# Attention stage of a two-layer trunk: value differences from PSUM, keys of two heads split at once, residual sums issued a unit later, low output parts ahead of a blanking

## Chip, cores, metric

The kernel runs on one core of a Trainium2 chip. The metric is the device time of one execution in microseconds, lower is better. Engines are named as in the profile: PE (matrix multiply), PEld (its weight load), DVE (vector), ACT (scalar), POOL (GpSimd), SP (the engine that here only issues DMAs).

## The reference

Two layers, float32, one batch of 1024 tokens, width 1024. Layer 0 mixes tokens with a short gated convolution, layer 1 with sliding-window attention; a SwiGLU block of 2816 hidden units follows each. The change lies in layer 1's attention:

```
q, k, v = split(rmsnorm(x) @ w_qkv)                  # 16 query heads, 4 key/value heads, 64 wide
q, k = rmsnorm(q), rmsnorm(k)                        # per head
for each block of 128 queries, against its own and the previous block of keys:
    s = q @ k.T / 8 - slope[head] * distance         # only 0 <= distance < 128
    p = softmax([s, sink[head]])[:-1]
    o = p @ v
x = x + o @ w_o
```

## The kernel before

All products are float32 in three passes: an operand is split into a high part (rounded to the matmul format) and a low part (what is left), and high*high, high*low and low*high are added in PSUM. PE has nearly no pause from end to end; everything else is arranged around it. The order of the instructions on each engine is written by hand: `line.work(n, f)` appends PE work and advances a planned clock `line.end`; `line.at(t, f)` puts an action of another engine (or a DMA) at planned time t. When the program is recorded, actions come out in the order of t, and each engine runs its own in that order; a planned time is never waited for.

The attention runs in 32 units, `unit(u)`: block of queries b = u // 4, half of the heads c = u // 2 % 2, key head g = u % 2 within it. A unit holds the stages of three units at once, so that PE always has something to do:

- `scores(u)` on PE into the PSUM bank `twin`; `merge`, `bias`, `least` on DVE; `exponents` on ACT; `inverse` (reciprocal of the sum) on DVE; `normal` (the product with the reciprocal) on POOL.
- `turn(u-1)`: PE transposes the probabilities, so it needs `normal(u-1)`. Then `turn_hi` (ACT), `turn_lo` (DVE), and `select` (POOL, the "blanking": four `affine_select`, two on the high part, two on the low part).
- `values(u-2)` and `other_values(u-2)` on PE: the probabilities times v of one block, and the blanked ones times the difference of v between this block and the one before. Then `o_copy` (ACT) and `o_add` (DVE).
- `o_hi` (ACT) and `o_lo` (POOL): the split of finished outputs, needed only in the output product after the units.

Between these, PE works on pieces of three matmuls: the query and key/value projections of later blocks, and from unit 24 on the output product (`tail_piece`). Eight pieces make an output tile m; it ends in `tail_item`, which adds the tile to X (loaded again by `load_again` from unit 27 on), squares it (ACT), stores it (a DMA issued by POOL) and sums the squares (DVE).

For a block b, `dv_sum` made the difference v(b) - v(b-1) in `scratch()` from the split parts, in three POOL instructions spread over units 4b-3 to 4b-1; `dv_hi`, `dv_lo` and `dv_twice` split it in unit 4b and copied it to the other 64 partitions. For the keys of two heads, `key_turn` (PE) transposes them to 128 partitions, 64 for each head; `key_hi` and `key_lo` split each head by itself, and `key_twice` copies each to the other 64 partitions.

Of the kernel before, what the change touches and what calls it, by code (L numbers as in the profile page):

```python
# [12 lines left out]
AF = mybir.ActivationFunctionType  # L13
ALU = mybir.AluOpType
# [56 lines left out]
def trunk_kernel(ctx: ExitStack, tc: tile.TileContext, xT, small, table, w_in, w_out, w_kv, w_q, w_o, w_gu, w_dn, out):  # L71
# [38 lines left out]
    def plain(ap):  # L110
        return ap.bitcast(F32)
# [676 lines left out]
    class Line:  # L788
# [216 lines left out]
    def channel_mixer(layer, next_stage, src_of, operands, raw_tags, extra_tags, slots, line, lead_in):  # L1005
# [61 lines left out]
        def tail_item(h, m, k0=0):  # L1067
            c = slice(h * HALF, h * HALF + HALF)
            tail_part(h, m, range(k0, n_op))
            get = tails[h, m][1]  # L1070
            t = line.end

            def square():
                if layer and h == 0 and m == 0:
                    units["sq"] = slot("A2", (P, 3, HALF))
                if m == 0:
                    state["ss", h] = units["sq"][:, 2] if layer and h == 0 else slot(f"s{h}", (P, HALF))
                    act.activation(state["ss", h], X[m][:, c], AF.Square)
                else:
                    if layer and h == 0:  # L1080
                        units["sq", h, m] = units["sq"][:, m % 2]
                    else:
                        units["sq", h, m] = slot(f"G{10 + m % 2}", (P, HALF))
                    act.activation(units["sq", h, m], X[m][:, c], AF.Square)

            at(t + 0.05, lambda: dve.tensor_tensor(X[m][:, c], get(), X[m][:, c], ALU.add))
            at(t + 0.8, square)
            at(t + 0.9, lambda: nc.gpsimd.dma_start(xres[m][:, c], X[m][:, c]))
            if m:
                at(t + 1.6, lambda: dve.tensor_tensor(state["ss", h], state["ss", h], units["sq", h, m], ALU.add))  # L1090


        B, put = operands_of(line, slots)
# [460 lines left out]
    def attention_layer(line, mixer):  # L1554
# [150 lines left out]
        def scratch():  # L1705
            return side_room(0)[:, NKV * HD :].rearrange("p (g d) -> p g d", d=HD)
# [56 lines left out]
        def key_hi(b, c, g):  # L1763
            rows = slice(g * HD, (g + 1) * HD)
            act.activation(key_rooms(c)[rows, g, 0, b % 2, :], KT[b, c][rows, 0:P], AF.Copy, scale=state["qkg"][rows])

        def key_lo(b, c, g):
            rows = slice(g * HD, (g + 1) * HD)
            kz = key_rooms(c)
            dve.scalar_tensor_tensor(  # L1770
                kz[rows, g, 1, b % 2, :],
                KT[b, c][rows, 0:P],
                state["qkg"][rows],
                plain(kz)[rows, g, 0, b % 2, :],
                ALU.mult,
                ALU.subtract,
            )

        def key_twice(b, c, g):
            rows, rest = slice(g * HD, (g + 1) * HD), slice((1 - g) * HD, (2 - g) * HD)  # L1780
            kz = key_rooms(c)
            nc.sync.dma_start(plain(kz)[rest, g, :, b % 2, :], plain(kz)[rows, g, :, b % 2, :])


        def dv_sum(b, i):
            d, v, w = scratch(), plain(v_room(b + 1)), plain(v_room(b))
            if i == 0:
                pool.tensor_tensor(d, v[:, :, 0, :], w[:, :, 0, :], ALU.subtract)
            elif i == 1:
                pool.tensor_tensor(d, d, v[:, :, 1, :], ALU.add)  # L1790
            else:
                pool.tensor_tensor(d, d, w[:, :, 1, :], ALU.subtract)

        def v_down(b, n=HD):
            nc.sync.dma_start(plain(v_room(b))[0:n], plain(v_room(b + 1))[0:n])
# [218 lines left out]
        def lead_in(tail_part, tail_item):  # L2014
# [4 lines left out]
            for b in (0, 1):  # L2019
                d = t + (-0.6, 0.1)[b]  # L2020
                at(d, kv_v_hi, b)
                at(d + 0.5, kv_v_lo, b)
                if b == 0:
                    at(d + 1.5, v_down, 0, P)
                at(d + 1.0, kv_square, b)
# [21 lines left out]
            def turn_keys(b, c, t_hi, t_lo):  # L2047
                line.work(small_turn, key_turn, b, c)
                t_hi = line.end + 0.05 if t_hi is None else t_hi
                t_lo = line.end + 0.5 if t_lo is None else t_lo  # L2050
                for g in (0, 1):
                    at(t_hi, key_hi, b, c, g)
                    at(t_lo, key_lo, b, c, g)
                    at(t_lo + 0.6, key_twice, b, c, g)

            def turn_query(m, t_hi, t_lo):
                line.work(4 * small_turn, q_turn, m)
# [42 lines left out]
            def unit(u, last):  # L2100

                s = line.end
                n, g = u // 2, u % 2
                b, c = n // 2, n % 2
                todo = deque(fill[u] if u < NU else [])
# [38 lines left out]
                if 0 <= u - 2 < NU:  # L2144
                    if u - 2 >= 4:
                        line.work(4 * 0.27, other_values, u - 2)
                    at(line.end + 0.05, o_copy, u - 2)
                    at(max(line.end + 0.7, s + 4.0), o_add, u - 2)
                    if g == 1:
                        at(s + 6.7, o_hi, n - 1)  # L2150
                        if n - 1 < 14:
                            at(s + 6.5 + 5.0, o_lo, n - 1, (0, 1))
                            at(s + 13.0 + 5.0, o_lo, n - 1, (2, 3))
                        else:
                            at(s + 7.6, o_lo, n - 1)
                if 4 <= u - 1 < NU:
# [20 lines left out]
                if g == 1 and n < 12 and n % 2:  # L2177
                    kb = n // 2 + 2
                    for d, f in (
                        (3.55, kv_v_hi),  # L2180
                        (4.9, kv_v_lo),
                        (6.0, kv_square),
                        (6.4, kv_sum),
                        (7.0, kv_mean),
                        (7.1, kv_guess),
                        (7.6, kv_newton),
                        (6.5 + 5.2, kv_scale),
                    ):
                        at(s + d, f, kb)
                if b + 1 < NB and u % 4:  # L2190
                    at(s + 4.9, dv_sum, b + 1, u % 4 - 1)
                if b and u % 4 == 0:
                    at(s + 0.2, v_down, b)
                    at(s + 0.3, dv_hi, b)
                    at(s + 4.6, dv_lo, b)
                    at(s + 6.4, dv_twice, b)


            def load_again(m):
# [127 lines left out]
```

## Time and profile before

| | us |
|---|---|
| median of 3 runs | 1902.4 (1902.19 to 1902.78) |
| the profiled execution, its own time | 1902.64 |
| its span, first to last instruction | 1900.9 |
| attention units, start of unit 0's scores to start of unit 31's | 988.8 to 1194.6 |

In the rows of the profile, L1937 is `turn`, L1977 `other_values`, L1968 `values`, L1888 `scores`, L1845 the transposes of the queries that stand ahead of `turn` in even units, L1653 to L1655 a projection piece, L1061 to L1063 an output piece; on POOL L1931 is `normal`, L1959 `select`, L2011 `o_lo`, L1788 to L1792 `dv_sum`, L1807 its half of `dv_lo`; on DVE L1927 is `inverse`, L1731 `kv_v_lo`, L1086 the addition to X, L1090 the sum of squares, L1856 `q_lo`, L1998 `o_add`. A time row has start, duration, engine, line, operation, tiles, shape and count; the bracket is idle time before it and what ended it. A matmul of 512 columns is shown 0.39 us long, but the next one starts some 0.23 us after it: PE is read by starts.

### The profile page before, as it was taken

What the parts mean: (1) busy time and instruction counts of PE and PEld (TensorE: products, weight loads), DVE (VectorE), ACT (ScalarE), POOL (GpSimd) and SP (SyncE); (2) the same over time, 40 slices, a digit from 0 to 9 for tenths busy, and PEclk for the clock granted to TensorE, in tenths of its full rate; (3) what the DMA queues carried; (4) which work ended last, traced back from release to release, by engine and by line L of the source; (5) the groups of instructions that cost most, each with busy time, mean ns of one, the idle gap of its engine ahead of it and who ended that gap; (6) DMA issues with size and microseconds to landing.
All of it is one profiled execution on the core that took longest, in us unless ns stands there. A gap on an engine that the chain in (4) does not pass through costs nothing.

```text
span 1900.9 us, 24865 instructions
## 1 busy us (share of the span) xinstructions
PE 1891.5 (100%) x8603; PEld 1567.9 (82%) x8603; DVE 1372.0 (72%) x2233; ACT 852.2 (45%) x1710; POOL 330.4 (17%) x634
## 2 busy tenths in 40 slices
PE   9999999999999999999999999999999999999999
PEld 7888888888888888888888887888888888888887
DVE  8997878868777777766678888468767676765543
ACT  5543444523333344444557777335333333344441
POOL 0000011012222221000016777300111111100000
PEclk9999999999999999999999999999999999999999
DMA  8522176146666667987730115744454654477563
GB/s 312 174 95 78 67 293 216 60 168 225 218 229 214 224 208 244 359 292 235 239 115 22 25 38 171 280 168 138 150 188 150 215 188 162 165 282 263 196 228 101
DMA packets 160254, 351.38 MB, mean 185 GB/s; under 512 B 15936, under 2 KB 60352, under 8 KB 160000
## 3 DMA queue, kind: packets, MB, share of 16 engines
q1 hardware_dynamic: 133632, 256.83, 40.4%
q0 software_dynamic: 26208, 92.81, 13.4%
q8 instruction: 67, 1.10, 0.2%
q14 instruction: 59, 0.48, 0.1%
q10 hardware_dynamic: 288, 0.16, 0.0%
HBM read 241.34 MB, written 103.28 MB: 181 GB/s over the span
## 4 chain that ended last, share of the span: by engine, by line
PE 90%; POOL 3%; DVE 3%; ACT 2%; issue 1%; DMA 1%; SPq 0%; DVEq 0%; POOLq 0%; ACTq 0%
PE acc L946 16%; PE acc L947 16%; PE acc L948 16%; PE P L946 9%; PE P L947 9%; PE P L948 9%; PE acc L1061 2%; PE acc L1062 2%; PE acc L1063 2%; PE acc L175 1%; PE P L1653 1%; PE P L1655 1%; PE P L1654 1%; POOL G L1959 1%; POOL G L1931 1%
## 5 line engine op out<-in xcount | busy, mean ns | idle before, releaser
L946 PE MATMUL acc<-XS,G 128*128 128x512 f32 x880 | 342.5, 389 | 0.0
L948 PE MATMUL acc<-XS,G 128*128 128x512 f32 x880 | 342.4, 389 | 0.0
L947 PE MATMUL acc<-XS,G 128*128 128x512 f32 x880 | 342.3, 389 | 0.0
L946 PEld LDWEIGHTS acc<-XS,G 128*128 128x128 f32 x880 | 165.2, 188 | 34.3
L947 PEld LDWEIGHTS acc<-XS,G 128*128 128x128 f32 x880 | 165.2, 188 | 34.3
L948 PEld LDWEIGHTS acc<-XS,G 128*128 128x128 f32 x880 | 165.2, 188 | 34.2
L946 PE MATMUL P<-A,G 128*128 128x512 f32 x476 | 185.3, 389 | 0.0
L947 PE MATMUL P<-A,G 128*128 128x512 f32 x476 | 185.2, 389 | 0.0
L948 PE MATMUL P<-A,G 128*128 128x512 f32 x476 | 185.2, 389 | 0.0
L946 PE MATMUL acc<-A,G 128*128 128x512 f32 x441 | 171.7, 389 | 0.0
L948 PE MATMUL acc<-A,G 128*128 128x512 f32 x441 | 171.4, 389 | 0.0
L947 PE MATMUL acc<-A,G 128*128 128x512 f32 x441 | 171.4, 389 | 0.0
L882 DVE TENSOR_TENSOR G<-WL,G 128x512 fp32r<-128x512 f32 x168 | 116.9, 696 | 47.8 <-ACT G L881 47.8
L881 ACT CAST G<-WR 128x512 fp32r<-128x512 f32 (+1 forms) x200 | 120.9, 605 | 60.9 <-PE acc L948 28.7
L882 DVE TENSOR_TENSOR G<-WR,G 128x512 fp32r<-128x512 f32 (+1 forms) x200 | 133.2, 666 | 9.3 <-ACT G L881 8.9
L881 ACT CAST G<-WH 128x512 fp32r<-128x512 f32 (+1 forms) x158 | 94.9, 601 | 82.8 <-PE acc L948 34.2
L1232 ACT ACTIVATE G<-G 128x512 f32<-128x512 f32 x88 | 55.8, 634 | 159.9 <-DVE G L1303 155.8
L946 PE MATMUL P<-XS,G 128*128 128x512 f32 x316 | 123.0, 389 | 0.1
L881 ACT CAST G<-WL 128x512 fp32r<-128x512 f32 x168 | 103.6, 617 | 43.3 <-DVE WL L821 38.7
L948 PE MATMUL P<-XS,G 128*128 128x512 f32 x316 | 122.9, 389 | 0.0
L947 PE MATMUL P<-XS,G 128*128 128x512 f32 x316 | 122.9, 389 | 0.0
L882 DVE TENSOR_TENSOR G<-WH,G 128x512 fp32r<-128x512 f32 (+1 forms) x158 | 106.4, 673 | 6.5 <-ACT G L881 6.4
(334 smaller groups left out, 3820.8 us busy)
## 6 DMA issues: line engine op xcount, KB each, us to landing
G<-h SPq DMA_DIRECT2D x70, 512.0 KB, 5.3
h<-X POOLq DMA_DIRECT2D x44, 512.0 KB, 5.4
X<-in_w_dn SPq DMA_DIRECT2D x80, 256.0 KB, 3.7
s<-X POOLq DMA_DIRECT2D x40, 512.0 KB, 4.4
WR<-in_w_gu SPq DMA_DIRECT2D x36, 512.0 KB, 5.8
WH<-in_w_gu SPq DMA_DIRECT2D x36, 512.0 KB, 6.4
h<-X POOLq DMA_DIRECT2D x66, 256.0 KB, 3.9
WR<-s SPq DMA_DIRECT2D x54, 256.0 KB, 3.1
```

The costliest lines, as they stand in the source:

```text
L175: pe.matmul(ps.half(h), wh, xs[:, j, c], start=first and j == 0, stop=False)
L881: lambda: act.copy(out_hi, raw),
L882: lambda: lo_eng.tensor_tensor(out_lo, raw, plain(out_hi), ALU.subtract),
L946: pe.matmul(ps[:, q], w[:, 0, c], x[:, 0, q], start=start and e == 0, stop=False, skip_group_check=True)
L947: pe.matmul(ps[:, q], w[:, 0, c], x[:, 1, q], start=False, stop=False, skip_group_check=True)
L948: pe.matmul(ps[:, q], w[:, 1, c], x[:, 0, q], start=False, stop=last, skip_group_check=True)
L1061: pe.matmul(ps, hi[:, kc], xs[:, 0, c], start=k == 0, stop=False, skip_group_check=True)
L1062: pe.matmul(ps, hi[:, kc], xs[:, 1, c], start=False, stop=False, skip_group_check=True)
L1063: pe.matmul(ps, lo[:, kc], xs[:, 0, c], start=False, stop=k == n_op - 1, skip_group_check=True)
L1232: state["silu"] = act.activation(x, x, AF.Silu)
L1653: pe.matmul(ps, x[:, 0, t], hi, start=k == 0, stop=False)
L1654: pe.matmul(ps, x[:, 0, t], lo, start=False, stop=False)
```

## The change

- Value differences: `whole_sum` adds the high and low part of v(b) in one POOL instruction; when v(b+1) is in PSUM, `dv_sum` makes r*v(b+1) minus that sum in one DVE instruction. `dv_hi`, `dv_lo` and `dv_twice` move from unit 4b to unit 4b-2, and `dv_lo`'s POOL half now stands behind `normal`.
- Keys: `key_hi` and `key_lo` split both heads in one instruction each on 128 partitions, into the second head's room; `key_halves` then makes three copies in place of two. The third overwrites what the first two read.
- Residual: in units 27 to 30 the addition to X, its square, its store and the sum of squares of a finished output tile get planned times in the next unit.
- Low output parts: `o_lo` is planned 1.2 us earlier, which puts it between the two halves of the blanking.

```diff
+            later = state.pop("tail_at", None)
+            t = later or line.end
...
             at(t + 0.05, lambda: dve.tensor_tensor(X[m][:, c], get(), X[m][:, c], ALU.add))
             at(t + 0.8, square)
-            at(t + 0.9, lambda: nc.gpsimd.dma_start(xres[m][:, c], X[m][:, c]))
+            at(t + (2.6 if later else 0.9), lambda: nc.gpsimd.dma_start(xres[m][:, c], X[m][:, c]))
             if m:
-                at(t + 1.6, lambda: dve.tensor_tensor(state["ss", h], ...))
+                at(t + (4.3 if later else 1.6), lambda: dve.tensor_tensor(state["ss", h], ...))
...
+        def key_hi(b, c):
+            act.activation(key_rooms(c)[:, 1, 0, b % 2, :], KT[b, c][:, 0:P], AF.Copy, scale=state["qkg"])
+        def key_lo(b, c):
+            kz = key_rooms(c)[:, 1, :, b % 2, :]
+            dve.scalar_tensor_tensor(kz[:, 1], KT[b, c][:, 0:P], state["qkg"], plain(kz)[:, 0], ALU.mult, ALU.subtract)
+        def key_halves(b, c):
+            first, second = (plain(key_rooms(c))[:, g, :, b % 2, :] for g in (0, 1))
+            nc.sync.dma_start(first[HD:P], second[0:HD])
+            nc.sync.dma_start(first[0:HD], second[0:HD])
+            nc.sync.dma_start(second[0:HD], second[HD:P])
+        def whole_sum(b):
+            v = plain(v_room(b + 1))
+            pool.tensor_tensor(scratch(), v[:, :, 0, :], v[:, :, 1, :], ALU.add)
+        def dv_sum(b):
             dve.scalar_tensor_tensor(
+                scratch(), kv_heads(b, 1), tok["r"][:, b : b + 1], scratch(), ALU.mult, ALU.subtract
             )
-        def dv_sum(b, i):
-            d, v, w = scratch(), plain(v_room(b + 1)), plain(v_room(b))
-            if i == 0:
-                pool.tensor_tensor(d, v[:, :, 0, :], w[:, :, 0, :], ALU.subtract)
-            elif i == 1:
-                pool.tensor_tensor(d, d, v[:, :, 1, :], ALU.add)
-            else:
-                pool.tensor_tensor(d, d, w[:, :, 1, :], ALU.subtract)
...
                 else:
+                    state["tail_at"] = state["next"]
                     tail_item(0, m, k)
...
                 s = line.end
+                state["next"] = s + 11.2 if u + 1 < NU else None
...
-                            at(s + 6.5 + 5.0, o_lo, n - 1, (0, 1))
+                            at(s + 6.5 + 3.8, o_lo, n - 1, (0, 1))
...
-                if b + 1 < NB and u % 4:
-                    at(s + 4.9, dv_sum, b + 1, u % 4 - 1)
+                if b + 1 < NB and u % 4 == 2:
+                    at(s + 0.3, dv_hi, b + 1)
...
+                    if b + 2 < NB:
+                        at(s + 6.4, whole_sum, b + 1)
```

What it does to the order of the instructions, at three places. The first is POOL from unit 8 on, up to `normal(8)` (the last row; G_1238 holds the probabilities, G_1257 the blanked ones, XS the outputs' low parts). Before:

```order
L1908 COPY G_1238_8231<-cst_64 128x4
L1959 AFFINE_SELECT G_1257_8347<-G_1256_8346 64x256 x4
L1807 TENSOR_TENSOR G_1323_8869<-G_1221_8140,G_1323_8869 64x4x64
L2011 TENSOR_TENSOR XS_1146_7710<-s_1266_8420,XS_1146_7710 128x128
L2011 TENSOR_TENSOR XS_1153_7738<-s_1266_8420,XS_1153_7738 128x128
L1931 TENSOR_TENSOR G_1238_8231<-G_1238_8231,at_d_8923 128x4x128
```

The same place in the changed kernel:

```order
L1901 COPY G_1238_8231<-cst_64 128x4
L1952 AFFINE_SELECT G_1257_8347<-G_1256_8346 64x256 x2
L2004 TENSOR_TENSOR XS_1146_7710<-s_1267_8422,XS_1146_7710 128x128
L2004 TENSOR_TENSOR XS_1153_7738<-s_1267_8422,XS_1153_7738 128x128
L1952 AFFINE_SELECT G_1257_8347<-G_1256_8346 64x256 x2
L1924 TENSOR_TENSOR G_1238_8231<-G_1238_8231,at_d_8920 128x4x128
```

`dv_lo` is gone from here and `o_lo` went between the two pairs of selects.

The second is DVE in unit 11, from `turn_lo` to `inverse(11)`, where the next block's keys and values are prepared. Before:

```order
L1952 TENSOR_TENSOR G_1256_8346<-acc_1360_9154,G_1256_8346 128x512
L1998 TENSOR_TENSOR s_1266_8420<-acc_1357_9136,s_1266_8420 64x512
L1839 TENSOR_TENSOR s_1363_9187<-P_1343_9004,at_y_9133 128x512
L1731 SCALAR_TENSOR_TENSOR G_1210_8091<-P_1333_8941,r_7905,G_1210_8091 128x4x64
L1927 RECIPROCAL at_d_9173<-at_d_9173 128x4
```

In the changed kernel (L1783 is the new `dv_sum`):

```order
L1945 TENSOR_TENSOR G_1256_8346<-acc_1360_9152,G_1256_8346 128x512
L1991 TENSOR_TENSOR s_1267_8422<-acc_1357_9134,s_1267_8422 64x512
L1783 SCALAR_TENSOR_TENSOR G_1213_8101<-P_1333_8939,r_7905,G_1213_8101 128x256
L1832 TENSOR_TENSOR s_1363_9188<-P_1343_8998,at_y_9131 128x512
L1732 SCALAR_TENSOR_TENSOR G_1210_8091<-P_1333_8939,r_7905,G_1210_8091 128x4x64
L1920 RECIPROCAL at_d_9171<-at_d_9171 128x4
```

One DVE instruction more stands ahead of the reciprocal.

The third is DVE in unit 27, from `least(27)` on; the X in the second row is output tile 0, loaded at the start of that unit. Before:

```order
L1916 TENSOR_REDUCE at_x_10532<-G_1238_8231 128x4
L1086 TENSOR_TENSOR X_1525_10496<-P_1499_10309,X_1525_10496 128x512
L1856 TENSOR_TENSOR G_1523_10492<-P_1517_10437,G_1523_10492 64x512
L1952 TENSOR_TENSOR G_1256_8346<-acc_1532_10534,G_1256_8346 128x512
L1998 TENSOR_TENSOR s_1266_8420<-acc_1529_10516,s_1266_8420 64x512
L1839 TENSOR_TENSOR s_1536_10570<-P_1507_10354,at_y_10513 128x512
L1927 RECIPROCAL at_d_10556<-at_d_10556 128x4
```

In the changed kernel, from the row after `least(27)` on:

```order
L1849 TENSOR_TENSOR G_1523_10477<-P_1517_10422,G_1523_10477 64x512
L1945 TENSOR_TENSOR G_1256_8346<-acc_1532_10519,G_1256_8346 128x512
L1991 TENSOR_TENSOR s_1267_8422<-acc_1529_10501,s_1267_8422 64x512
L1832 TENSOR_TENSOR s_1535_10553<-P_1507_10336,at_y_10498 128x512
L1920 RECIPROCAL at_d_10537<-at_d_10537 128x4
L1890 COPY_PREDICATED twin_10559<-cst_64,twin_10559 128x4x128
L1896 TENSOR_TENSOR G_1238_8231<-twin_10559,A_1194_7996 128x4x128
L1909 TENSOR_REDUCE at_x_10589<-G_1238_8231 128x4
L1769 SCALAR_TENSOR_TENSOR G_1231_8182<-P_1540_10591,qkg_7769,G_1231_8182 128x128
L1945 TENSOR_TENSOR G_1256_8346<-acc_1542_10599,G_1256_8346 128x512
L1991 TENSOR_TENSOR G_1213_8101<-acc_1536_10574,G_1213_8101 64x512
L1087 TENSOR_TENSOR X_1525_10481<-P_1499_10295,X_1525_10481 128x512
```

The addition to X went eleven instructions down, from behind `least(27)` to behind `o_add` of unit 28.

More of the change, by code (lines that the diff above doesn't have):

```diff
@@ L1070, in tail_item @@
             get = tails[h, m][1]
-            t = line.end
+            later = state.pop("tail_at", None)
+            t = later or line.end
             def square():
@@ L1087, in tail_item @@
             at(t + 0.8, square)
-            at(t + 0.9, lambda: nc.gpsimd.dma_start(xres[m][:, c], X[m][:, c]))
+            at(t + (2.6 if later else 0.9), lambda: nc.gpsimd.dma_start(xres[m][:, c], X[m][:, c]))
             if m:
-                at(t + 1.6, lambda: dve.tensor_tensor(state["ss", h], state["ss", h], units["sq", h, m], ALU.add))
+                at(t + (4.3 if later else 1.6), lambda: dve.tensor_tensor(state["ss", h], state["ss", h], units["sq", h, m], ALU.add))
         B, put = operands_of(line, slots)
@@ L2023, in lead_in @@
                 if b == 0:
+                    at(d + 1.1, whole_sum, 0)
                     at(d + 1.5, v_down, 0, P)
+                else:
+                    at(d + 1.3, dv_sum, 1)
+                    d += 0.9
                 at(d + 1.0, kv_square, b)
@@ L2050, in turn_keys @@
                 t_lo = line.end + 0.5 if t_lo is None else t_lo
[L2051 to L2054, printed above, removed]
+                at(t_hi, key_hi, b, c)
+                at(t_lo, key_lo, b, c)
+                at(t_lo + 0.6, key_halves, b, c)
             def turn_query(m, t_hi, t_lo):
@@ L2151, in unit @@
                         if n - 1 < 14:
-                            at(s + 6.5 + 5.0, o_lo, n - 1, (0, 1))
-                            at(s + 13.0 + 5.0, o_lo, n - 1, (2, 3))
+                            at(s + 6.5 + 3.8, o_lo, n - 1, (0, 1))
+                            at(s + 13.0 + 3.8, o_lo, n - 1, (2, 3))
                         else:
@@ L2180, in unit @@
                         (3.55, kv_v_hi),
+                        (4.5, dv_sum),
                         (4.9, kv_v_lo),
@@ L2189, in unit @@
                         at(s + d, f, kb)
-                if b + 1 < NB and u % 4:
-                    at(s + 4.9, dv_sum, b + 1, u % 4 - 1)
+                if b + 1 < NB and u % 4 == 2:
+                    at(s + 0.3, dv_hi, b + 1)
+                    at(s + 2.3, dv_lo, b + 1)
+                    at(s + 4.0, dv_twice, b + 1)
+                    if b + 2 < NB:
+                        at(s + 6.4, whole_sum, b + 1)
                 if b and u % 4 == 0:
                     at(s + 0.2, v_down, b)
-                    at(s + 0.3, dv_hi, b)
-                    at(s + 4.6, dv_lo, b)
-                    at(s + 6.4, dv_twice, b)
             def load_again(m):
```

16 lines of the change are left out of this document (removed).

## Prediction

> **What bounds the kernel now.** I read the span, then the busy time by stretch, then PE's rows in the attention by their starts, and last the queue of whatever PE waits for.
>
> ```profile
> span 1900.9 us, 24865 instructions
> ```
>
> ```profile
> 700.00:950.00 250.00, 250.00 (x1105) 207.01 (x1104) 170.84 (x267) 116.07 (x183) 18.50 (x24) 1.00 0.78 269
> 995.00:1165.00 170.00, 169.07 (x930) 141.95 (x930) 142.54 (x253) 127.34 (x430) 125.92 (x306) 1.00 0.14 37
> 1165.00:1210.00 45.00, 42.32 (x222) 35.17 (x221) 30.70 (x52) 25.63 (x85) 31.32 (x65) 1.00 0.77 272
> ```
>
> The columns are the stretch, its length, and busy time of PE, PEld, DVE, ACT and POOL. Outside the attention PE has no idle time; in it 0.93 + 2.68 us. The change touches nothing else, and the number of matmuls stays, so a gain can only be time that PE loses there. Idle time is too small a measure of it, since a matmul row is shown longer than the distance to the next; I compare distances between starts. First the step from the last piece before `turn` (L1655) to `other_values` (L1977): unit 11, where nothing is late, and the first and last of five units 4b+1 (9, 13, 17, 21, 25).
>
> ```profile
> 1061.45 0.39 PE L1655 MATMUL P<-A,XS 128*128 128x512 f32 x1
> 1062.04 0.48 PE L1977 MATMUL acc<-G,G 128*128 128x256 f32 x2
> ...
> 1048.00 0.39 PE L1655 MATMUL P<-WH,XS 128*128 128x512 f32 x1
> 1048.87 0.36 PE L1977 MATMUL acc<-G,G 128*128 128x256 f32 x1
> ...
> 1154.87 0.39 PE L1655 MATMUL P<-A,XS 128*128 128x512 f32 x1
> 1155.78 0.48 PE L1977 MATMUL acc<-G,G 128*128 128x256 f32 x2
> ```
>
> 0.59 us in unit 11; 0.87 to 0.91 in the five: 0.28 to 0.32 lost in each, 1.5 together. In even units the query transposes (L1845) stand in front. Here are unit 12 and the first and last of six units 4b+2 (6, 10, 14, 18, 22, 26):
>
> ```profile
> 1068.03 0.60 PE L1845 MATMUL P<-cst,s 128*128 128x128 f32 x4
> 1068.88 0.48 PE L1977 MATMUL acc<-G,G 128*128 128x256 f32 x2
> ...
> 1027.94 0.60 PE L1845 MATMUL P<-cst,s 128*128 128x128 f32 x4
> 1029.15 0.48 PE L1977 MATMUL acc<-G,G 128*128 128x256 f32 x2
> ...
> 1161.76 0.60 PE L1845 MATMUL P<-cst,s 128*128 128x128 f32 x4
> 1162.72 0.48 PE L1977 MATMUL acc<-G,G 128*128 128x256 f32 x2
> ```
>
> 0.85 against 1.21 and 0.96: 0.36 and 0.11 lost, the six together 1.3. Both kinds wait for `normal` on POOL. Its queue and the reciprocal it needs, in unit 12:
>
> ```profile
> 1070.39 1.83 POOL L1959 TENSOR_SCALAR_AFFINE_SELECT G<-G 64x256 fp32r<-64x256 f32 x4
> 1072.30 0.79 POOL L1807 TENSOR_TENSOR G<-G,G 64x256 fp32r<-64x256 f32 x1
> 1073.17 0.89 POOL L2011 TENSOR_TENSOR XS<-s,XS 128x128 fp32r<-128x128 f32 x2
> 1074.01 1.04 POOL L1931 TENSOR_TENSOR G<-G,at_d 128x512 f32<-128x512 f32 x1
> ```
>
> ```profile
> 1072.86 0.17 DVE L1927 RECIPROCAL at_d<-at_d 128x4 f32<-128x4 f32 x1
> ```
>
> The reciprocal is there at 1073.03; POOL starts at 1074.01 because `dv_lo` (0.79) and `o_lo` (0.89) are ahead of it. In units 4b+1 `dv_sum` takes `dv_lo`'s place.
>
> The second loss is in units 27 to 29. The chain and DVE's row, then PE in unit 28 beside the same stretch of unit 24, and PE in unit 29:
>
> ```profile
> 1165.75 5.89 DMA X<-xmid
> ```
>
> ```profile
> 1171.74 0.69 DVE L1086 TENSOR_TENSOR X<-P,X 128x512 f32<-128x512 f32 x1 [1.54 <-DMA X<-xmid]
> ```
>
> ```profile
> 1145.33 1.12 PE L1888 MATMUL twin<-G,G 128*128 128x256 f32 x8
> 1146.75 0.39 PE L1653 MATMUL P<-X,XS 128*128 128x512 f32 x1
> ...
> 1171.97 0.40 PE L1888 MATMUL twin<-G,G 128*128 128x256 f32 x2
> ...
> 1175.23 0.39 PE L1061 MATMUL P<-XS,WH 128*128 128x512 f32 x1
> ...
> 1176.72 0.60 PE L1845 MATMUL P<-cst,s 128*128 128x128 f32 x4
> ...
> 1178.01 0.36 PE L1977 MATMUL acc<-G,G 128*128 128x256 f32 x1
> ...
> 1183.65 0.39 PE L1063 MATMUL P<-XS,WL 128*128 128x512 f32 x1
> ...
> 1185.30 0.48 PE L1977 MATMUL acc<-G,G 128*128 128x256 f32 x2
> ```
>
> DVE stands at the addition to X until the load lands; `q_lo` and `o_add` behind it release the scores and `values`. That stretch takes 3.26 us against 1.42: 1.84 lost. Then 1.29 against 0.85 (0.44 lost) and 1.65 against 0.59 (1.06 lost): 3.3 in all.
>
> **The change, part by part.**
>
> *POOL.* In units 4b the 0.79 of `dv_lo` leaves the stretch ahead of `normal`, in units 4b+1 one `dv_sum` of 0.74 (L1788 to L1792 differ little). `o_lo` (0.89) is not removed, but goes ahead of the second pair of selects, which wait for `turn_lo`; in units 4b+1 POOL idles there. `normal` can then start at the reciprocal or when the queue is through: in unit 12 the queue gives 1070.39 + 1.83 + 0.89 + gaps of 0.1, about 1073.2, so 0.8 earlier where PE loses 0.3. Units 4b+1 gain 0.74 plus up to the idle time, where PE loses 0.11 to 0.36. Both losses go: -2.8. `dv_lo` comes back behind `normal` of unit 4b+1, `whole_sum` (one addition of `dv_sum`'s size, 0.74) behind `normal` of 4b+2; behind both stand only the little instructions of the query norm and selects that wait for ACT. I cost them at nothing; without that cover each would push the next selects by under 0.8, and through them the next `normal`, whose new slack is about as large.
>
> *DVE's new `dv_sum`.* Its shape and its PSUM operand are those of `kv_v_lo`, 0.48 us:
>
> ```profile
> 1119.73 0.48 DVE L1731 SCALAR_TENSOR_TENSOR G<-P,r,G 128x256 fp32r<-128x256 f32 x1
> 1120.12 0.17 DVE L1927 RECIPROCAL at_d<-at_d 128x4 f32<-128x4 f32 x1
> ```
>
> ```profile
> 1120.99 1.04 POOL L1931 TENSOR_TENSOR G<-G,at_d 128x512 f32<-128x512 f32 x1
> ```
>
> ```profile
> 1122.08 0.66 PE L1937 MATMUL acc<-cst,G 128*128 128x128 f32 x4
> ```
>
> It stands ahead of `inverse` in six units 4b+3, which then ends at 1120.29 + 0.48 = 1120.77 in this unit. `normal` started at 1120.99 behind `dv_sum` and `o_lo`; without the one, and with the other moved, it can start at 1120.9. It ends just when `turn` begins, so this is the tightest place: between 0.1 gained and, if the DVE queue adds its whole 0.48 to the reciprocal and POOL gives nothing back, 6 x 0.4 = 2.4 lost. I take 0, by the two rows above.
>
> *`dv_hi`, `dv_lo`, `dv_twice` two units earlier.* ACT's two conversions now stand behind `exponents` of unit 4b+1, where ACT waits for DVE's `o_add` next; DVE's half delays `least` of 4b+2, whose follower `exponents` comes after `turn_hi` and `o_copy` anyway. The copies are used two units later than that. Nothing.
>
> *Keys.* One ACT and one DVE instruction replace two each, a gain off the path, since the next on both engines waits for `turn`. On SP each key costs three copies, and the third waits until the first two have landed.
>
> ```profile
> DMA to landing us min/median/max: 2.0/2.1/4.0
> ```
>
> ```profile
> 1163.11 1.42 SPq L1782 DMA_DIRECT2D G<-G  x2
> ```
>
> So a first head is ready some 2.9 us after the low part (issued 0.7 apart, landing 2.1 after the second issue) and a second head 5, where the scores that read them come two and three units (13 us or more) later. In the lead-in they come soonest:
> ```profile
> 983.01 0.73 DVE L1770 SCALAR_TENSOR_TENSOR G<-P,qkg,G 64x128 fp32r<-64x128 f32 x2 [1.61 <-ACT G L1765]
> ```
>
> The first half of this pair ends at 983.4, so the first room is ready by 986.3 and the second by 988.4; unit 0's scores start at 988.8 and unit 1's, the second room's readers, a unit later. What is queued behind the wait on SP in unit 26: both `dv_twice` copies, the weights of output tile 2, X0 and X1. By the rows their issue goes from 1165.75 to about 1169, and X0 lands at 1169 + 5.89 = 1175.
>
> *Residual.* The addition of tile 0 moves behind `o_add` of unit 28, to where tile 1's stands now:
>
> ```profile
> 1180.76 0.69 DVE L1086 TENSOR_TENSOR X<-P,X 128x512 f32<-128x512 f32 x1
> ```
>
> Without the stall of 2.3 us in this unit (1.84 + 0.44) and the `dv_lo` that stood ahead of it, DVE is there at about 1178: X0 has 3 us to spare. So the 1.84 goes, and with it 0.44 and 1.06, which were its followers: exponents behind the square, and the store ahead of `normal` in unit 28, which now comes after. -3.3.
>
> The sum of squares moves too, in unit 31 ahead of `turn_lo`, while POOL is at `select`:
>
> ```profile
> L1959 POOL TENSOR_SCALAR_AFFINE_SELECT G<-G x112: 407/412/964, 1023.1 to 1206.7; 64x256 fp32r<-64x256 f32 x112
> ```
>
> A select can run long (0.96 for 0.41), and the one that does already lies ahead of the last `normal`. So the cost is 0 to 0.55, and I take 0: the collision moves from one select of that unit to the other. The Trainium skill (SBUF — State Buffer, Who interferes with whom) says that a DVE instruction with two SBUF inputs and a GpSimd instruction that reads SBUF exclude each other, the later one blocking until the other is through. The long row agrees; by that rule taken at its worst the gain would be 0.55 smaller, and the time 1896.9.
>
> *Sum* against the profiled execution's own time: 1902.64 - 2.8 - 3.3 = 1896.5. That execution is 0.24 above the median of 1902.4, so **1896.3**.
>
> Which measure of PE's loss is right decides the sum: idle rows of 0.93 + 2.68 = 3.6 would give 1898.8. The Trainium skill (Perfetto Trace Analysis, Identifying the Most-Contended Engine) calls the matmul row's busy share a poor measure because matmuls are pipelined; the trace agrees, with 0.39 shown where the next starts after 0.23.
>
> **Rivals.** (1) *The stall moves on.* X0 waits behind the third key copy and DVE stands at the addition in unit 28. For it: a load took 5.89 among others, and starts 3 us later. Against it: 3 us to spare. From a landing after 1178 on each us costs one; at 3.3 only the loop's 2.8 are left: 1899.6. (2) *The reciprocal takes over.* In six units `dv_sum` delays `inverse` and `turn` waits in unit 4b+4: at most 2.4 lost, 1898.7. For it: no slack in the rows above; against it: POOL's 0.74 ahead of `normal` goes in just these units. (3) *Slower.* The weights of output tile 2 stand in the same SP queue, and PE needs them at unit 28's fifth piece, about 1177 (1.42 after the scores' start at 1171.97, then four pieces of three matmuls at 0.23, and 1.3 for the transposes). Issued at 1168, they are late if they take over 9 us, and only past 15 is the whole 6.1 used up. The trace's loads of 5.89 speak against it; at 16 us it would be 1903. (4) *No effect*: `normal` is early, but `turn_lo` or `o_add` hold PE instead, 1902. PE's own rows name POOL and the X load, which speaks against it.
>
> **How the numbers follow.** Forecast 0.64, rivals (1) 0.12, (2) 0.12, (3) 0.05, (4) 0.03, other things 0.04. The forecast's own range is 1895.3 (if the small excess goes too that units 4b and 32 show in the same reading, some 0.9) to 1897.5. The range takes in rivals (1) and (2): 1895.0 to 1900.2. About 0.2% (3.8 us) is what a measurement of this kernel can tell from no change; the line is at 1898.6. The forecast and a partial (1) or (2) lie below it, their full forms above: faster 0.70, same 0.23, slower 0.07.
>
> **What would show it.** Right: PE's step from L1655 to `other_values` back at about 0.59 in units 9 to 25, and in unit 28 no idle time at the scores; DVE's addition to X without a wait for the load; `normal` starting within 0.2 of `inverse`. Wrong: `turn` later in units 12, 16, 20, 24 (rival 2); DVE idle at the addition in unit 28 (1); output pieces waiting for wo (3). A pause of some us on PE in the lead-in would mean that I misjudged the key copies.

## The result and the profile after

| | before | after |
|---|---|---|
| median of 6 runs, us | 1902.26 (1902.01 to 1902.78) | 1894.86 (1894.54 to 1895.31) |
| the profiled execution, own time and span | 1902.64, 1900.9 | 1894.54, 1892.8 |
| start of unit 0's scores to start of unit 31's | 205.80 | 198.24 |
| start of unit 31's scores to the end of the span | 706.37 | 706.28 |

The ratio is 0.9961, with a 95% interval of 0.9948 to 0.9974: 7.4 us faster. All of it lies in the 31 units, which got 7.56 us shorter. Unit 0 also starts 0.46 us earlier, but the two traces are 0.48 apart 8 us after the start already, where the programs are the same; over the kernels below that start varies between 988.23 and 989.17. The forecast of 1896.3 was 1.4 us short of the gain, and the time lies 0.14 below the low end of the range, 1895.0.

The span, and the stretches of busy time (stretch, length, busy time of PE, PEld, DVE, ACT and POOL):

```profile
span 1892.8 us, 24868 instructions
```

```profile
995.00:1165.00 170.00, 170.00 (x953) 146.63 (x952) 142.79 (x253) 123.99 (x427) 120.61 (x303) 1.00 0.17 45
1158.00:1203.00 45.00, 44.77 (x239) 38.00 (x238) 31.46 (x53) 26.60 (x88) 29.78 (x65) 1.00 0.79 281
```

PE's idle time of 0.93 and 2.68 us in these two stretches of the program is down to nothing and 0.23. By starts, the steps to `other_values` (now L1970; a piece is L1654 to L1656, the query transposes L1838): units 13 and 12.

```profile
1072.82 0.39 PE L1656 MATMUL P<-WH,XS 128*128 128x512 f32 x1
...
1073.40 0.48 PE L1970 MATMUL acc<-G,G 128*128 128x256 f32 x2
...
1066.41 0.60 PE L1838 MATMUL P<-cst,s 128*128 128x128 f32 x4
...
1067.20 0.48 PE L1970 MATMUL acc<-G,G 128*128 128x256 f32 x2
```

0.58 us in unit 13, where the units 4b+1 had 0.87 to 0.91. In unit 12 it is 0.79, where the prediction took 0.85 for "nothing is late": that unit had itself waited for 0.06. POOL and the reciprocal (L1920) in front of unit 13 (L1952 `select`, L2004 `o_lo`, L1924 `normal`):

```profile
1068.19 0.89 POOL L1952 TENSOR_SCALAR_AFFINE_SELECT G<-G 64x256 fp32r<-64x256 f32 x2
1069.17 0.88 POOL L2004 TENSOR_TENSOR XS<-s,XS 128x128 fp32r<-128x128 f32 x2
1070.12 0.87 POOL L1952 TENSOR_SCALAR_AFFINE_SELECT G<-G 64x256 fp32r<-64x256 f32 x2
1071.07 1.04 POOL L1924 TENSOR_TENSOR G<-G,at_d 128x512 f32<-128x512 f32 x1
```

```profile
1070.19 0.18 DVE L1920 RECIPROCAL at_d<-at_d 128x4 f32<-128x4 f32 x1
```

`normal` starts 0.70 after the reciprocal, not within 0.2 of it; it still ends at 1072.11, 0.94 ahead of `turn` at 1073.05. In unit 28 the scores (L1881) run through, and the addition to X (L1087) has no wait in front:

```profile
1167.34 1.12 PE L1881 MATMUL twin<-G,G 128*128 128x256 f32 x8
...
1173.51 0.69 DVE L1087 TENSOR_TENSOR X<-P,X 128x512 f32<-128x512 f32 x1
```

SP does wait for its third key copy (L1775), and longer than the prediction allowed. Its queue in unit 28:

```profile
1171.90 0.62 SPq L1774 DMA_DIRECT2D G<-G  x1
1177.82 0.59 SPq L1775 DMA_DIRECT2D G<-G  x1
1178.46 1.07 SPq L2201 DMA_DIRECT2D X<-xmid  x2
```

From the end of the one issue to the start of the next 5.3 us pass, with the loads of X2 and X3 behind them. These landed at 1182.0 and 1183.7, 4 us or more ahead of the additions that use them (1185.95 and 1189.85).

What the sum lacked is found by unit lengths (distance of the scores' starts): the units 4b, of which the prediction expected nothing, went from 6.97 to 6.75. The 0.22 us stood at two places. One is `turn`, in the prediction's own reading; unit 20 before and after:

```profile
1121.61 0.60 PE L1845 MATMUL P<-cst,s 128*128 128x128 f32 x4
1122.49 0.48 PE L1977 MATMUL acc<-G,G 128*128 128x256 f32 x2
...
1118.33 0.60 PE L1838 MATMUL P<-cst,s 128*128 128x128 f32 x4
1119.12 0.48 PE L1970 MATMUL acc<-G,G 128*128 128x256 f32 x2
```

0.88 against 0.79: in each of the five units 4b 0.06 to 0.10 was lost there, 0.4 together. The other place is the first piece on WR. Unit 20 before, with the row of PE's own queue for that line, `key_lo` (L1770) and PE. The first row counts the semaphore instructions ahead of that piece, five, the last at 1124.1 in unit 20; its 51 ns are the instruction's own time, not the wait's:

```profile
L1653 PEldq EVENT_SEMAPHORE  x5: 51/51/51, 1017.5 to 1124.1; - x5
```

```profile
1123.36 0.73 DVE L1770 SCALAR_TENSOR_TENSOR G<-P,qkg,G 64x128 fp32r<-64x128 f32 x2 [0.18 <-ACT G L1765]
```

```profile
1123.98 0.39 PE L1655 MATMUL P<-X,XS 128*128 128x512 f32 x1
1124.24 0.47 PE L1653 MATMUL P<-WR,XS 128*128 128x512 f32 x1
1124.55 0.39 PE L1654 MATMUL P<-WR,XS 128*128 128x512 f32 x1
```

After, in the same unit:

```profile
1120.06 0.34 DVE L1769 SCALAR_TENSOR_TENSOR G<-P,qkg,G 128x128 fp32r<-128x128 f32 x1
```

```profile
1120.58 0.39 PE L1656 MATMUL P<-X,XS 128*128 128x512 f32 x1
1120.81 0.39 PE L1654 MATMUL P<-WR,XS 128*128 128x512 f32 x1
1121.04 0.39 PE L1655 MATMUL P<-WR,XS 128*128 128x512 f32 x1
```

The key transposes are written into a PSUM bank that this piece takes next. Before, the second `key_lo` read it until 1124.10 and the piece began at 1124.24, with 0.26 and 0.31 us to its neighbours in place of 0.23. After, there is one `key_lo`, done at 1120.40, and the steps are 0.23. That is 0.12 us in unit 20 and 0.6 in the five; the last 0.1 of the 1.1 is spread over small steps. Matmul rows of 0.39 cover such a wait: no idle time of PE is shown.

### The profile page after: what moved, and what is told of

Read it like the earlier page. It is cut to its first block, busy times and chain, and to the rows that moved or that the text cites. A ratio compares the mean times of both kernels' runs of the same rounds, so it can differ in the third digit from the quotient of the medians.

```text
span 1892.8 us, 24868 instructions
## 1 busy us (share of the span) xinstructions
PE 1887.4 (100%) x8603; PEld 1569.8 (83%) x8603; DVE 1368.5 (72%) x2224; ACT 844.4 (45%) x1694; POOL 319.1 (17%) x620
## 4 chain that ended last, share of the span: by engine, by line
PE 98%; DVE 1%; issue 0%; DMA 0%; ACT 0%; POOL 0%; DVEq 0%; ACTq 0%
PE acc L946 16%; PE acc L948 16%; PE acc L947 16%; PE P L946 9%; PE P L948 9%; PE P L947 9%; PE P L1654 2%; PE P L1656 2%; PE P L1655 2%; PE acc L1061 2%; PE acc L1062 2%; PE acc L1063 2%; PE twin L1881 2%; PE acc L175 1%; PE acc L1961 1%; PE acc L1930 1%
```

## The experiments

The change has four parts, and every one was taken out of the changed kernel and put into the kernel before by itself. Mean unit lengths in us, from one profile each (units 4b: 8 to 24; 4b+1: 9 to 25; 4b+2: 10 to 26). The kernel before was timed again beside each group, with medians of 1902.1 to 1902.9, and the ratios are to these:

| kernel | median | ratio to before, 95% interval | 4b | 4b+1 | 4b+2 | 28 | 29 | 30 | units 0 to 31 |
|---|---|---|---|---|---|---|---|---|---|
| before | 1902.26 | | 6.97 | 6.53 | 7.00 | 9.11 | 7.28 | 6.21 | 205.80 |
| after | 1894.86 | 0.9961 (0.9948 to 0.9974) | 6.75 | 6.23 | 6.75 | 6.75 | 6.23 | 6.24 | 198.24 |
| after, old keys | 1896.76 | 0.9969 (0.9957 to 0.9981) | 7.08 | 6.24 | 6.77 | 6.77 | 6.23 | 6.23 | 200.45 |
| after, old residual times | 1902.25 | 0.9998 (0.9989 to 1.0007) | 6.77 | 6.23 | 6.77 | 13.31 | 6.23 | 6.21 | 205.10 |
| after, old o_lo time | 1895.47 | 0.9961 (0.9948 to 0.9973) | 6.75 | 6.23 | 6.75 | 6.75 | 6.23 | 6.43 | 198.47 |
| after, old differences | 1901.63 | 0.9993 (0.9984 to 1.0002) | 6.75 | 6.99 | 6.77 | 6.75 | 6.41 | 8.96 | 205.22 |
| before, new keys | 1903.66 | 1.0008 (0.9999 to 1.0016) | 6.76 | 6.62 | 6.76 | 11.63 | 7.29 | 6.23 | 206.44 |
| before, new residual times | 1899.50 | 0.9986 (0.9977 to 0.9995) | 6.95 | 6.50 | 7.01 | 6.82 | 6.24 | 6.67 | 202.84 |
| before, new o_lo time | 1901.38 | 0.9993 (0.9985 to 1.0002) | 7.07 | 6.68 | 6.75 | 8.55 | 7.22 | 6.21 | 205.24 |
| before, new differences | 1903.81 | 1.0005 (0.9996 to 1.0014) | 7.10 | 6.24 | 6.75 | 11.51 | 6.20 | 7.49 | 206.36 |

The four alone change the units by +0.64 (keys), -2.96 (residual), -0.56 (`o_lo`) and +0.56 (differences), -2.3 in all; together it is -7.56. Three of them by themselves run into waits that another part removes. Two of the means hold one long unit: unit 9 with 7.39 in "after, old differences" (the other four 6.89 to 6.92), and unit 8 with 7.51 in "before, new o_lo time" (the others 6.91 to 6.98, as before).

**After with the old keys.** The edit puts `key_hi`, `key_lo` and `key_twice` of each head back.

> The changed kernel with the old keys (key_hi, key_lo and a copy for each head). Theory (the second key_lo holds a PSUM bank): with two key_lo of 0.34 the bank that the first piece of the next projection writes comes free about 5.4 us after the start of units 4b, as in the kernel before, and PE waits there again for 0.13 us; six units, so 0.8 us slower than the changed kernel: 1895.7, units 4b at 6.88 instead of 6.75, all others unchanged. Rival (the prediction's own line, keys are off the path): no unit changes, 1894.9.

The bank's wait is there, in units 4b and nowhere else, but of 0.33 us rather than 0.13. The late `turn` of units 4b is gone, so PE comes to the bank sooner, while `key_lo` ends no earlier (5.47 us into unit 20, 5.40 in the kernel before): the two waits overlapped before. Beside the other parts the keys are worth 2.2 us by the units and 1.9 by the medians.

**After with the old residual times.** The edit takes `later` out of `tail_item`.

> The changed kernel without the later planned times of the residual sums. Theory: the stall at the addition to X comes back and is larger than before, because the third key copy and the earlier dv_twice issue X0's load some 3.3 us later in unit 27 than before (3.3 us after its start instead of at it): 3.3 us of the old stall and up to 3.3 more, 1901.5 (1899.5 to 1902). Rival: the landing does not follow the issue (the queue was not what held it), so only the old 3.3 come back: 1898.2.

```profile
1164.59 0.86 SPq L2198 DMA_DIRECT2D X<-xmid  x2
```

```profile
1171.33 0.69 DVE L1086 TENSOR_TENSOR X<-P,X 128x512 f32<-128x512 f32 x1 [5.71 <-DMA X<-xmid]
```

```profile
1172.89 1.62 PE L1880 MATMUL twin<-G,G 128*128 128x256 f32 x6 [4.92 <-DVE G L1848]
```

As expected: unit 28 loses 6.56 us, twice the old 3.4 of units 28 and 29. X0's load is issued late by the third key copy and the earlier `dv_twice`, and without the later addition the whole change would have been worth nothing.

**After with o_lo at its old time.** `at(s + 6.5 + 5.0, o_lo, ...)` and `at(s + 13.0 + 5.0, ...)` again.

> The changed kernel with o_lo planned at its old time. Theory (redundant beside the value differences): POOL's queue ahead of normal is short enough without it; in unit 14 normal would end 0.3 us later than in the changed kernel, still 0.8 us ahead of turn. No unit changes, 1894.9 (within 0.3). Rival (it is needed, as the prediction had it): turns late again in units 4b+2, 0.1 to 0.4 us each, 1896.2.

No unit of the loop changes. The median is 0.6 us above the changed kernel's, twice what was allowed; the profile shows 0.2 in unit 30, where `turn` is late, and 0.3 behind the start of unit 31. In the loop this move is redundant beside the new differences, as the theory had it, but not in the last units.

**After with the old differences.** The three `dv_sum` on POOL and the split in units 4b are back.

> The changed kernel with the old value differences (three subtractions and additions on POOL, the split in unit 4b). Theory: in units 4b ACT has one key_hi less ahead of turn_hi, so the selects and normal come 0.39 us earlier than in the kernel before, where turn in units 4b+1 came 0.37 late; in units 4b+2 o_lo fills the time in which POOL waited. All turns are in time or within 0.1: 1894.9 to 1895.4. Rival (the prediction: dv_lo and dv_sum ahead of normal are what holds PE): 0.3 us come back in each of five units 4b+1, and some in 4b+2: 1896.4 to 1897.5.

Both expectations missed, by much. `normal` (L1924) of unit 12 ends 10.10 us after that unit's start, where it ended 9.94 after it before, and since units 4b are 0.2 shorter, `turn` (L1930) is wanted earlier and waits longer. ACT, POOL and PE of unit 12 and the start of 13:

```profile
1066.71 0.42 ACT L1792 ACTIVATE G<-G 64x256 fp32r<-64x256 f32 x1
1067.13 0.40 ACT L1793 CAST G<-G 64x256 fp32r<-64x256 f32 x1
...
1068.68 0.20 ACT L1686 ACTIVATE at_y<-at_y 128x4 f32<-128x4 f32 x1
```

```profile
1068.97 0.20 POOL L1690 TENSOR_TENSOR at_t<-at_y 128x4 f32<-128x4 f32 x1 [0.92 <-ACT at_y L1686]
...
1070.11 0.89 POOL L1952 TENSOR_SCALAR_AFFINE_SELECT G<-G 64x256 fp32r<-64x256 f32 x2
...
1073.24 0.74 POOL L1800 TENSOR_TENSOR G<-G,G 64x256 fp32r<-64x256 f32 x1
1074.06 1.04 POOL L1924 TENSOR_TENSOR G<-G,at_d 128x512 f32<-128x512 f32 x1
```

```profile
1075.15 0.66 PE L1930 MATMUL acc<-cst,G 128*128 128x128 f32 x4 [0.46 <-POOL G L1924]
```

My theory that `turn_hi` on ACT sets the selects fell: they stand behind the little instructions of the key norm (L1690 is the first), which wait for ACT's guess (L1686), and that stands behind the two `dv_hi` (L1792, L1793). So the new differences help twice in this place, by `dv_lo` (L1800) off POOL and by `dv_hi` off ACT; no run took the two apart. The second loss, 2.7 us in unit 30, is new. The `dv_twice` of that kernel (L1804) still stands in unit 28, behind the third key copy, and PE waits for it at `other_values`:

```profile
1180.93 0.59 SPq L1775 DMA_DIRECT2D G<-G  x1
...
1182.85 0.49 SPq L1804 DMA_DIRECT2D G<-G  x1
```

```profile
1190.33 0.74 PE L1970 MATMUL acc<-G,G 128*128 128x256 f32 x2 [2.17 <-DMA G<-G]
```

**Before with the new keys alone.**

> The kernel before with the new keys alone. Theory: the bank wait in units 4b goes (0.8 us), turn_hi comes 0.39 us earlier there, so the late turns of units 4b+1 go too (1.5 us); but the third copy makes X0's load 1.7 us later, and the stall in unit 28 grows by as much: 1902.3 - 0.8 - 1.5 + 1.7 = 1901.7, with unit 28 at about 10.8 (9.1 before). Rival (keys off the path, third copy hidden): 1902.3, no unit changes.

Units 4b are at 6.76, nothing of their loss is left: the bank is free, and `turn` is in time too (the reciprocal ends 1.41 us into unit 20 and `normal` 3.15, before 1.60 and 3.33). Units 4b+1 are not mended but longer, for the reason just told: `turn` is wanted earlier. Unit 28 grows by 2.5 rather than 1.7, so that the part alone is no gain, where 0.6 was expected.

**Before with the new residual times alone.**

> The kernel before with the later planned times of the residual sums alone. Theory: only units 28 and 29 change, to 6.75 to 6.9 and 6.2 to 6.3: 3.3 us less, 1898.9. Rival (the stall moves on to the later addition): unit 28 keeps part of its loss, 1900 or more.

As expected in units 28 and 29 (3.3 us less); unit 30 gives 0.46 back, where `turn` is late.

**Before with the new o_lo time alone.**

> The kernel before with o_lo planned 1.2 us earlier alone. Theory: in units 4b+2 POOL waited 1.1 us for turn_lo between the two pairs of selects; o_lo fills it and their late turns go (1.6 us); in units 4b+1 POOL did not wait there, so the late turns of 0.3 stay: 1900.7, units 4b+1 unchanged at 6.5. Rival (the prediction's reading, POOL's queue is simply shorter): both go, 1899.2; or neither, 1902.3.

Units 4b+2 from 10 on go to 6.75, and units 4b+1 do not gain: POOL's idle time between the two pairs of selects is what the move uses. They even lose 0.15.

**Before with the new differences alone.**

> The kernel before with the new value differences alone. Theory: the late turns of units 4b+1, 4b+2 and 4b all go (1.5, 1.6 and 0.4 us), the bank wait of units 4b stays, and the two dv_twice copies, now issued in unit 26 ahead of X0's load, make that 1.2 us later and the stall in unit 28 as much longer: 1902.3 - 3.5 + 1.2 = 1900.0. Rival: the new dv_sum on DVE delays the reciprocal, turns in units 4b+4 are late by up to 0.4: 1902 or more.

Units 4b+1 and 4b+2 are mended, and no reciprocal is late. But units 4b go up to 7.10 (PE meets the bank sooner, as in the first experiment), and unit 28 to 11.51 by `dv_twice` ahead of X0's load, 2.4 rather than 1.2 more; unit 30 loses another 1.3. Alone this part brings nothing.

**The bank by itself, in the changed kernel.** One DVE instruction of 0.34 us more in units 4b: a second, identical `key_lo`, or as control one that reads SBUF and writes a free place there (`spare`, its definition left out here).

```diff
             dve.scalar_tensor_tensor(kz[:, 1], KT[b, c][:, 0:P], state["qkg"], plain(kz)[:, 0], ALU.mult, ALU.subtract)
+            if b and c:      # held
+                dve.scalar_tensor_tensor(kz[:, 1], KT[b, c][:, 0:P], state["qkg"], plain(kz)[:, 0], ALU.mult, ALU.subtract)
+            if b and c:      # the control, in a kernel of its own
+                dve.scalar_tensor_tensor(spare, plain(kz)[:, 0], state["qkg"], plain(kz)[:, 0], ALU.mult, ALU.subtract)
```

> The changed kernel with the key_lo of the second key head pair issued twice (the same instruction, same result), 0.34 us more of DVE that reads the PSUM bank. Theory (the bank is what the old keys cost): the bank comes free 5.4 us after the start of units 4b instead of 5.0, PE waits for it at the first piece of the next projection by 0.3 us, units 4b 7.05 to 7.1 instead of 6.75 and all others unchanged: 1894.9 + 6 x 0.32 = 1896.8. Rival (it was the key copies or ACT's second key_hi, and the bank has slack): no unit changes, 1894.9.

> The control of the run before it: the same 0.34 us of DVE at the same place, but reading SBUF and writing a spare place, so that the PSUM bank is free as early as in the changed kernel. Theory: units 4b stay at 6.75, 1894.9. Rival (what counts is DVE's time ahead of turn_lo, not the bank): units 4b as long as in the run before it, 1896.8.

Held, unit 20:

```profile
1121.41 0.35 DVE L1771 SCALAR_TENSOR_TENSOR G<-P,qkg,G 128x128 fp32r<-128x128 f32 x1
```

```profile
1121.60 0.39 PE L1656 MATMUL P<-X,XS 128*128 128x512 f32 x1
1121.82 0.49 PE L1654 MATMUL P<-WR,XS 128*128 128x512 f32 x1
1122.15 0.40 PE L1655 MATMUL P<-WR,XS 128*128 128x512 f32 x1
```

Control, unit 20:

```profile
1121.43 0.39 PE L1656 MATMUL P<-X,XS 128*128 128x512 f32 x1
1121.65 0.39 PE L1654 MATMUL P<-WR,XS 128*128 128x512 f32 x1
1121.88 0.39 PE L1655 MATMUL P<-WR,XS 128*128 128x512 f32 x1
```

Held: 1896.68 (ratio 0.9969, 0.9957 to 0.9981), units 4b 6.91. Control: 1895.37 (0.9962, 0.9948 to 0.9975), units 4b 6.75 as in the changed kernel. The same DVE time costs nothing if it leaves the bank alone, so it is the bank. The size, 0.16, is half of what I expected: by estimate (0.35 added, 0.16 lost) the changed kernel has some 0.2 us of slack there. That the median came out near the forecast of 1896.8 is luck: the units grew by 1.1 us, not 1.9.

**The bank in the kernel before.** The same two edits there, in one half of the second pair.

> The kernel before with the last key_lo of units 4b issued twice (same result), 0.36 us more of DVE that reads the PSUM bank. Theory (the bank already held PE in units 4b of the kernel before, without any slack): each of the units 8, 12, 16, 20 and 24 gets longer by the whole 0.36, from 6.94-6.99 to about 7.3, and unit 4 too: 1902.3 + 2 = 1904.3, less what the later turn of units 4b+1 gains by it (up to 0.3 each, 1.5 in all). Rival (units 4b lost their 0.2 by the late turn alone, the bank had slack): units 4b longer by 0.2 or less.

> The control of the run before it: the kernel before with the same 0.36 us of DVE that reads SBUF only. Theory: units 4b stay at 6.94-6.99; turn_lo is 0.36 later there, and the late turns of units 4b+1 may grow by up to that: 1902.3 to 1904. Rival (what counts in units 4b is DVE's time): units 4b as long as in the run before it.

Held (L1779 is the added instruction), unit 20:

```profile
1123.95 0.36 DVE L1779 SCALAR_TENSOR_TENSOR G<-P,qkg,G 64x128 fp32r<-64x128 f32 x1
```

```profile
1123.80 0.39 PE L1655 MATMUL P<-X,XS 128*128 128x512 f32 x1
1124.45 0.47 PE L1653 MATMUL P<-WR,XS 128*128 128x512 f32 x1 [0.26 <-DVE G L1779]
```

Control:

```profile
1124.30 0.39 PE L1655 MATMUL P<-X,XS 128*128 128x512 f32 x1
1124.58 0.47 PE L1653 MATMUL P<-WR,XS 128*128 128x512 f32 x1
```

Held, units 4b go from 6.97 to 7.36, by 0.39: the whole 0.36 counts, so the kernel before had no slack at this bank. With the control they stay at 6.96, and its 0.36 appears in units 4b+1 (6.88). Here the trace names DVE as the releaser, since the wait outgrew the 0.39 of the row. The times, 1902.58 (1.0000, 0.9991 to 1.0009) and 1903.10 (1.0005, 0.9996 to 1.0014), do not tell the two apart; the lengths do.

**The reciprocal's slack.** `kv_v_lo` twice in units 4b+3, as if `dv_sum` cost double.

```diff
                         (4.9, kv_v_lo),
+                        (4.91, kv_v_lo),
```

> The changed kernel with kv_v_lo issued twice in units 4b+3: 0.48 us more of DVE ahead of the reciprocal, as if the new dv_sum cost double. In the changed kernel normal ends 0.33 us ahead of turn in units 4b. Theory (that is all the slack there is): turn 0.15 late and 0.06 for the restart after a wait, units 4b at 6.95 to 7.1 (the later merge and key_lo may also hold the bank), unit 4 at 7.2: 1896.0 to 1896.8. Rival (POOL or something else releases turn there and the reciprocal has slack): 1894.9.

1897.78 (0.9975, 0.9964 to 0.9986), 1.0 above the range; the units of the profile, whose own time was 1896.82, grew by 2.1. Units 4b are at 7.08: `turn` 0.24 to 0.34 late with its restart. So rival (2)'s mechanism is real, and the changed kernel stays clear of it by about 0.3 us.

**Mending what is left.** Two waits remain in the changed kernel: `turn(3)` in unit 4 (0.19) and `turn(31)` in unit 32 (0.45).

```diff
-                    at(e + 5.1, inverse, u)
+                    at(s + 4.45 if u % 4 == 3 and n < 12 else e + 5.1, inverse, u)
...
-                for _ in range(3 if u == NU else 2):
+                for _ in range(4 if u == NU else 2):
...
-                    for _ in range(6):
+                    for _ in range(5 if u == NU else 6):
```

> The changed kernel with the reciprocal of units 4b+3 planned ahead of dv_sum, kv_v_lo and the query scale, and with four output pieces ahead of the last turn instead of three. Theory: the two waits left in the attention go, turn(3) in unit 4 (0.19 us) and turn(31) in unit 32 (0.45 us), so 0.6 us less than the changed kernel: 1894.2, unit 4 at 6.53. Rival: the earlier reciprocal pushes kv_v_lo or the scale into another wait, or the output product ends no earlier: 1894.9 or more.

1896.56 (0.9968, 0.9955 to 0.9980), slower than the changed kernel. The reciprocal ahead of `dv_sum` waits for the exponents, and the 0.28 + 0.18 us pass down DVE's queue to `key_lo`: the bank again. Units 4b are at 6.99 to 7.01 for it, and unit 24 at 7.36, where DVE's `bias` also waited 0.47 for POOL; the reciprocal at the start of unit 12, and unit 24's first piece behind the bank:

```profile
1064.44 0.18 DVE L1920 RECIPROCAL at_d<-at_d 128x4 f32<-128x4 f32 x1 [0.28 <-ACT G L1915]
```

```profile
1148.43 0.50 PE L1061 MATMUL P<-XS,WR 128*128 128x512 f32 x1 [0.32 <-DVE G L1769]
```

**The last turn alone.** Only the second and third edit of those.

> The changed kernel with four output pieces ahead of the last turn instead of three, and nothing else. Theory: turn(31)'s wait of 0.45 us goes and all units stay as in the changed kernel: 1894.4. Rival (it was this edit that made units 4b of the mended kernel longer, or the output product then waits for the last outputs): 1894.9 or more.

The last `turn`, in the changed kernel and in this one:

```profile
1195.68 0.66 PE L1930 MATMUL acc<-cst,G 128*128 128x128 f32 x4 [0.23 <-POOL G L1924]
```

```profile
1196.08 0.60 PE L1930 MATMUL acc<-cst,G 128*128 128x128 f32 x4
```

1894.46 (0.9960, 0.9946 to 0.9973): start of unit 31 to the end 705.79 instead of 706.28, all units as in the changed kernel. It is the fastest of these kernels, by 0.4 us in the medians, less than timing alone can tell.

## Why the prediction was right, and where it was short

- **Late turns in units 4b+1: right.** Predicted 1.5, measured 5 x 0.30 = 1.5. Of the causes it gave, the differences mattered and `o_lo`'s move did not (alone it left these units late). It missed that `dv_hi` leaving ACT lets the key norm and the selects come earlier; no run shows what that is worth by itself.
- **Late turns in units 4b+2: right, 0.35 too small.** Predicted 1.3, measured 1.65. The term was mis-sized by its baseline: the 0.85 of unit 12, taken as a unit where nothing is late, held a wait of 0.06 itself, and six units were measured against it.
- **The stall of units 28 and 29: right.** Predicted 3.3, measured 3.4. That the load would be issued about 3 us later and do no harm was right too: X0 landed at 1171.04, 2.5 us ahead of its addition, where 3 were predicted. Without the later addition units 28 and 29 cost 6.6.
- **"Keys ... a gain off the path": wrong, and this is the step that failed.** It was costed at nothing, because the next work on ACT and DVE waits for `turn`. What it left out is PE, which takes the PSUM bank that `key_lo` reads for its next piece. Units 4b gained 5 x 0.22 = 1.1 us: 0.6 at the bank, 0.4 at `turn`, 0.1 in small steps. The keys by themselves bring nearly all of it (6.76), and without them units 4b are at 7.08. The 0.4 at `turn` goes with the differences alone as well, so it belongs to no one part; for `turn` in units 4b the prediction had allowed up to 0.1 gained in each and taken 0. The excess that it put into the low end of its range ("some 0.9", units 4b and 32) is this wait at `turn`, with no cause named; unit 32's part of 0.4 stayed. The bank it did not see: I read PE's starts around `turn` only, and never listed the other long steps.
- **Rivals.** (1) did not happen: X0 landed before the addition. (2) did not happen, with 0.3 us to spare. (3) did not happen either: SP stood longer than I assumed, but the loads behind it had time. Of the signs, `normal` within 0.2 of the reciprocal was wrong (0.70), since POOL's queue still ends later; PE did not need it sooner.

The sum: 1.5 + 1.65 + 3.4 + 1.1 = 7.65, and 0.1 given back in other units, is the 7.56 of the units, against 6.1 predicted. The 1.1 of units 4b and the 0.35 of the baseline are what was missing. The Trainium skill (Perfetto Trace Analysis, Optimization Strategy) says that the same gap repeated on the engine that should be saturated can mean there isn't enough SBUF or PSUM for the next tile. By that rule part of the excess of units 4b would have had a name, and the trace agrees for that part: some 0.12 us in each of five units, at a PSUM bank. But it also says to look for gaps between slices, and here PE's slices show none; only the distances do.

## What to carry to other kernels

List all start-to-start distances of the bounding engine against their median before pricing a change, and take each repeated excess down to the instruction that frees what is waited for; a part that is "off the path" for its own engines may hold a buffer that the bounding engine takes next. Waits at neighbouring places overlap, so parts of a change don't add: here three of the four alone bring at most 0.6 us in the units or lose, and the four together 7.6. In this kernel a copy that waits for copies on SP's queue delayed every load behind it (with the new keys alone, X0's load left 2.1 us later in unit 27), so move the users of these loads in the same change.

## What the hardware showed that was not expected

- After a wait, PE loses more than the wait: the matmul behind it is shown 0.47 to 0.50 us long and its follower starts 0.31 to 0.33 after it, against 0.39 and 0.23. Even a `turn` that came in time by start had 0.412 us to `other_values` instead of 0.355 when its input ended 0.05 us before it (unit 12 before, against unit 12 after).
- Small copies were slow behind big loads: in the changed kernel the first copy of the key halves (64 KB) landed 2.0 us after its issue in unit 26 and 6.3 after it in unit 28, where loads of X and wo (512 KB) issued before it were in flight and landed up to 1176.4; the third copy waited 1.5 and 5.3 us. That the loads are the cause is the likely reading; no run took them away.
